# Hybrid attention and expert layers: the scores of two heads take turns on the two row halves of TensorE

## The chip, the cores and the metric

One core of a Trainium2 chip runs the whole program. The metric is the device time of one execution in microseconds, the median of several runs. TensorE multiplies matrices, VectorE (DVE), ScalarE (ACT) and GpSimd (POOL) work elementwise, and SyncE (SP) issues most transfers.

## The reference

Two layers run on 512 tokens of width 1024 (a grid of 8 rows by 64 columns). A layer projects the normalised input, runs three groups of heads (A: neighbourhood attention, 6 heads of 64; B: latent attention, 6 heads; C: a gated short convolution), projects their normalised outputs back onto `x`, and then runs a router with 16 experts. The change is in group A:

```python
def one_row(args):
    r, q_row = args
    r0 = jnp.clip(r - wh // 2, 0, rows - wh)
    k_win = lax.dynamic_slice_in_dim(kg, r0, wh, axis=1)[:, :, col_idx]
    v_win = lax.dynamic_slice_in_dim(vg, r0, wh, axis=1)[:, :, col_idx]
    ...
    sc = jnp.einsum('bqhd,biqjhd->bhqij', q_row, k_win).astype(jnp.float32) * scale
    sc = sc + bias.astype(jnp.float32)[None]
    p = jax.nn.softmax(sc.reshape(b, h, GRID_W, wh * ww), axis=-1).reshape(sc.shape).astype(v.dtype)
    return jnp.einsum('bhqij,biqjhd->bqhd', p, v_win)
```

## The kernel before

A layer is a mixer (the three groups of heads and the projections, `mixer`) and then the experts (`moe`). The tokens are in 4 blocks of 128, each block a stripe of 16 grid columns, so that a block's neighbourhood keys lie in 2 or 3 blocks (`KEYS_OF`): 256 or 384 score columns with a mask (`MASK_AT`).

To keep precision, matrices of the mixer are split into a high and a low part, and a product is three matmuls into one PSUM tile (`mm3`, L151 to L154): high x high (L152), low x high (L153), high x low (L154). The names of these three lines therefore appear for projections and for scores alike.

`a_attn` (L626 to L677) is neighbourhood attention. It goes over 3 pairs of heads (`hp`), 4 blocks of queries (`j`) and the 2 heads of a pair (`hh`). The queries and keys of the two heads of a pair lie in one tile, the first head in partitions 0 to 63, the second in 64 to 127; a score matmul therefore contracts over 64 rows and uses one row half of the array. For each head: GpSimd makes the masked bias (L642, once for each mask), three score matmuls go into an `sc` bank, VectorE adds the bias and takes the minimum (L655), ScalarE takes the exponential (L657), VectorE normalises (L659, L660), TensorE transposes in 2 or 3 pieces (L663, into the one `pt` bank) and VectorE or ScalarE copies them out (L665). When both heads are done, the `po` matmuls (L671) multiply with the values; they use half of the columns. There are two `sc` banks, one `pt`, one `po` and four `prj` banks.

What else stands in the same stretch: the last projections of `a_prep` (`prj<-wring,hn`, 384 columns), the output projection in three parts (`out_part`, L703: `prj<-...`, 512 columns, added to `x` in L712), the loads of its weights (`wo_loads`, L685: transfers L691 into `fraw`, ScalarE's cast L698, GpSimd's remainder L699), and the normalisations of the groups (`group_norm`, L363: one matmul with ones in L367, then L369 to L375). `weave` (L171) mixes these as fills between the steps of `a_attn`, at each `yield`. The first part of the output projection needs the convolution, the second group B, the third group A, so its last part waits for the normalisation at the end of `a_attn`.

The order in which an engine executes is not that of the source: a scheduler sets it when the program is built, from the order of the source, from priorities (`first` raises the steps of the woven main generator by 60) and from its own estimate of when operands and banks are ready. Each engine then executes its list in order and waits where an operand is late.

Of the kernel before, what the change touches and what calls it, by code (L numbers as in the profile page):

```python
# [93 lines left out]
def build(tc, x_in, pp_in, con_in, gm_in, rpb_in, w_in, w_uq, w_ukv, w_out, w_gate, w_up, w_down, out,  # L94
# [3 lines left out]
    PE, ACT, DVE, POOL, SP = nc.tensor, nc.scalar, nc.vector, nc.gpsimd, nc.sync  # L98
# [6 lines left out]
    def tmp():  # L105
        return w2.tile([128, 512], F32, name="tmp", tag="tmp")

    def stat(n, tag="stat"):
        return st.tile([128, n], F32, name=f"{tag}{n}", tag=f"{tag}{n}")
# [41 lines left out]
    def mm3(ps, ah, al, bh, bl, first, last):  # L151
        PE.matmul(ps, ah, bh, start=first, stop=False)  # L152
        PE.matmul(ps, al, bh, start=False, stop=False)  # L153
        PE.matmul(ps, ah, bl, start=False, stop=last)  # L154
# [41 lines left out]
    def psum(pool, tag, bufs):  # L196
        return lambda: pool.tile([128, 512], F32, name=tag, tag=tag, bufs=bufs)
# [17 lines left out]
    def mixer(l, M, W, PSUM):  # L215
        def ptile():
            return W.tile([128, 512], F32, name="P", tag="P", bufs=7)

        def ftile():
            return W.tile([128, 512], F32, name="tmf", tag="tmf", bufs=2)  # L220
# [28 lines left out]
        def qkA(which, part):  # L249

            return qk[which](part * 1536, 1536).rearrange("p (h t) -> p h t", h=3)
# [26 lines left out]
        prj, sc, ptb, pob = (psum(psm, n_, b_) for n_, b_ in zip(("prj", "sc", "pt", "po"), (4, 2, 1, 1)))  # L278
# [76 lines left out]
        def squares(o, tot):  # L355

            ACT.activation(tot, o[0], AF.Square)
            for i in range(1, len(o)):
                sq = tmp()
                ACT.activation(sq, o[i], AF.Square)  # L360
                DVE.tensor_tensor(tot, tot, sq, op=OP.add)

        def group_norm(bank, o, tot, k0, mix):  # L363

            n = len(o)
            pn = bank()
            PE.matmul(pn, ones, tot, start=True, stop=True)  # L367
            ln = tmp()
            ACT.activation(ln, pn, AF.Ln, scale=1.0 / (n * 128), bias=eps)  # L369
            ACT.activation(ln, ln, AF.Exp, scale=-0.5)  # L370
            for i in range(n):
                DVE.scalar_tensor_tensor(o[i], o[i], P("gout", k0 + i), ln, op0=OP.mult, op1=OP.mult)
                hi, lo = mix[i]
                ACT.copy(hi, o[i])
                DVE.tensor_tensor(lo, o[i], f(hi), op=OP.subtract)  # L375
# [250 lines left out]
        def a_attn():  # L626
            for hp in range(3):
                bms = [{}, {}]
                po = pob()
                for j in range(NJ):  # L630
                    k0, k1 = KEYS_OF[j]
                    n = (k1 - k0) * 128
                    pts = []
                    for hh in range(2):
                        h = 2 * hp + hh
                        rows = slice(hh * 64, hh * 64 + 64)
                        if MASK_AT[j] not in bms[hh]:

                            bm = ptile()
                            b0 = k0 - j + 1  # L640
                            m0 = _C["mask"][0] + MASK_AT[j]
                            POOL.tensor_tensor(  # L642
                                bm[:, 0:n].rearrange("p (b k w) -> p b k w", k=WH, w=CB),
                                bias[:, h].rearrange("p (k b w) -> p b k w", k=WH, b=3)[:, b0:b0 + k1 - k0],
                                con[:, m0:m0 + n // WH].rearrange("p (b k w) -> p b k w", k=1, w=CB)
                                .to_broadcast([128, k1 - k0, WH, CB]), op=OP.add)
                            bms[hh][MASK_AT[j]] = bm
                        bm = bms[hh][MASK_AT[j]]
                        ps = sc()
                        q = [qkA(0, p)[rows, hp, j * 128:(j + 1) * 128] for p in range(2)]  # L650
                        k = [qkA(1, p)[rows, hp, k0 * 128:k1 * 128] for p in range(2)]
                        mm3(ps[:, 0:n], q[0], q[1], k[0], k[1], True, True)
                        p = ftile()
                        nm = stat(1)
                        DVE.tensor_tensor_reduce(p[:, 0:n], ps[:, 0:n], bm[:, 0:n], -1.0, 3.0e38, OP.add, OP.min, nm)  # L655
                        s_ = stat(1)
                        ACT.activation(p[:, 0:n], p[:, 0:n], AF.Exp, bias=nm, scale=-1.0, accum_out=s_)  # L657
                        rl = stat(1)
                        DVE.reciprocal(rl, s_)  # L659
                        DVE.tensor_scalar(p[:, 0:n], p[:, 0:n], rl, None, op0=OP.mult)  # L660
                        pt = ptb()
                        for i in range(k1 - k0):
                            PE.transpose(pt[:, i * 128:(i + 1) * 128], p[:, i * 128:(i + 1) * 128], ident)  # L663
                        pT = tmp()
                        (ACT.copy if hh else DVE.tensor_copy)(pT[:, 0:n], pt[:, 0:n])  # L665
                        pts.append(pT)
                        yield
                    for i in range(k1 - k0):
                        for hh in range(2):
                            h = 2 * hp + hh  # L670
                            PE.matmul(po[hh * 64:hh * 64 + 64, j * 128:(j + 1) * 128],  # L671
                                      va[:, k0 + i, h * DH:(h + 1) * DH], pts[hh][:, i * 128:(i + 1) * 128],
                                      start=i == 0, stop=i == k1 - k0 - 1)
                ACT.copy(oA[hp], po)
            tot = tmp()
            squares(oA, tot)
            group_norm(sc, oA, tot, 0, mixA)  # L677
# [43 lines left out]
        for r in range(8):  # L721
            ACT.dma_start(bias[r * CB:(r + 1) * CB], rpb_in[l, :, :, (7 - r) * 48:(15 - r) * 48])
        weave(a_attn(), 40, (wl, 3, 0), (o1, 3, 4),
              (norm_later(sc, oB, F(0, 512), 3, mixB), 1, 0), (wl, 1, 0), (o1, 5 - 3, 4), (wl, 1, 0), (o1, 4, 4),
              (wl, 1, 0), (o2, 3, 3), (wl, 1, 0), (o2, 3, 3), (wl, 1, 0), (o2, 3, 3), (wl, 1, 0))
# [48 lines left out]
        for i, _ in enumerate(o3):  # L774
            j = i // 2
# [250 lines left out]
```

## Time and profile before

| | us |
|---|---|
| median of 3 runs | 1595.0 |
| lowest and highest | 1593.73, 1596.5 |
| the profiled execution | 1593.64 |
| its span, first to last instruction | 1591.9 |
| TensorE busy in it | 1549.4 |

The profile is of one execution. Its views give for each engine the busy time, the instructions in order of time with their start and length, what ended an engine's idle time, and busy time by stretch. A matmul's length includes its way through the array, so consecutive matmuls overlap in the rows; how fast they follow each other is read from the distance of their starts. The mean granted clock of TensorE is 0.991 of full speed.

### The profile page before, as it was taken

The numbers are of one execution on the slowest core, as the hardware profiler recorded it, in microseconds if no ns is written. First come the engines' busy times: TensorE is split into PE (matmuls) and PEld (weight loads), VectorE is DVE, ScalarE is ACT, GpSimd is POOL, SyncE is SP. The second block draws the span as 40 slices with busy tenths as digits, with TensorE's granted clock in tenths as the row PEclk, the third lists the DMA queues.
The fourth block names the chain that finished last, engine by engine and source line by source line (L and its number), as shares of the span: only waits on it lengthen the run. The fifth ranks groups of instructions, "written<-read, shape, count | busy, mean of one in ns | idle before, by whom it ended". The sixth has DMA issues, their size and how long they took to land. (4 is left out here: it accounts for less than half of the span.)

```text
span 1591.9 us, 19849 instructions
## 1 busy us (share of the span) xinstructions
PE 1549.4 (97%) x7820; PEld 845.5 (53%) x7822; DVE 512.6 (32%) x1142; ACT 382.1 (24%) x937; POOL 232.8 (15%) x336
## 2 busy tenths in 40 slices
PE   7999999899999999999999999999999999999997
PEld 6877766544444444344388776674344344344342
DVE  5475466511201201211164744664012022022021
ACT  6465553210000000000165655431100000000000
POOL 4541450200000000000055325320000000000000
PEclk8999999999999999999999999999999999999999
DMA  4312125799999999999622221187999999999966
GB/s 164 85 48 63 56 71 202 290 375 389 410 409 409 408 409 409 409 409 382 212 69 71 64 57 67 41 316 273 392 389 409 409 409 409 409 409 409 409 269 211
DMA packets 138461, 441.74 MB, mean 277 GB/s; under 512 B 8832, under 2 KB 31360, under 8 KB 138368
## 3 DMA queue, kind: packets, MB, share of 16 engines
q1 hardware_dynamic: 136576, 438.11, 71.6%
q10 hardware_dynamic: 1792, 2.36, 0.5%
q8 instruction: 62, 1.02, 0.3%
q14 instruction: 31, 0.25, 0.1%
HBM read 438.33 MB, written 2.10 MB: 277 GB/s over the span
## 5 line engine op out<-in xcount | busy, mean ns | idle before, releaser
L898 PE MATMUL acc<-w,fmix 128*64 128x512 f32 x2944 | 651.1, 595 | 0.0
L898 PEld LDWEIGHTS acc<-w,fmix 128*64 128x64 f32 x2944 | 203.5, 137 | 391.8 <-issue 368.8
L947 DVE TENSOR_TENSOR x<-wk,x 128x512 f32<-128x512 f32 x128 | 87.1, 689 | 273.9 <-PE wk L946 272.7
L888 PEld LDWEIGHTS wk<-tmp,fmix 128*128 128x128 f32 x1024 | 119.8, 192 | 42.4 <-issue 42.4
L932 ACT ACTIVATE tmp<-acc 128x512 f32<-128x512 f32 x32 | 19.1, 597 | 464.8 <-PE acc L898 382.2
L888 PE MATMUL wk<-tmp,fmix 128*128 128x128 f32 x1024 | 128.2, 279 | 0.7 <-DVE tmp L880 0.7
L926 POOL COPY sel<-con 16x128 f32<-16x128 f32 x16 | 5.0, 318 | 806.4 <-PE wk L927 800.0
L946 PE MATMUL wk<-tmp 128*128 128x512 f32 x256 | 114.7, 599 | 1.6 <-ACT tmp L942 1.6
L317 POOL TENSOR_TENSOR wring<-fraw,wring 128x384 fp32r<-128x384 f32 (+1 forms) x88 | 91.4, 1047 | 139.7 <-ACT wring L316 134.4
L890 DVE TENSOR_TENSOR fmix<-wk,pp 128x256 f32<-128x256 f32 (+1 forms) x72 | 28.4, 395 | 218.2 <-PE wk L888 218.2
L946 PEld LDWEIGHTS wk<-tmp 128*128 128x128 f32 x256 | 47.1, 190 | 68.9 <-issue 41.6
L153 PE MATMUL prj<-wring,hn 128*128 128x384 f32 (+1 forms) x224 | 80.6, 360 | 0.8 <-DVE hn L296 0.8
L152 PE MATMUL prj<-wring,hn 128*128 128x384 f32 (+1 forms) x224 | 79.8, 358 | 0.3 <-ACT wring L316 0.3
L154 PE MATMUL prj<-wring,hn 128*128 128x384 f32 (+1 forms) x224 | 79.3, 354 | 0.1
L942 ACT ACTIVATE tmp<-acc,stat 128x512 f32<-128x512 f32 x32 | 22.0, 687 | 214.5 <-PE acc L898 176.7
L933 DVE TENSOR_TENSOR tmp<-acc,tmp 128x512 f32<-128x512 f32 x32 | 22.1, 691 | 135.1 <-PE acc L898 135.1
L922 DVE COPY stat<-wk 64x1 f32<-64x1 f32 x32 | 5.0, 156 | 177.7 <-PE wk L919 177.5
L937 ACT COPY fmix<-wk 128x512 f32<-128x512 f32 x32 | 18.8, 587 | 179.1 <-PE wk L936 179.1
L316 ACT CAST wring<-fraw 128x384 fp32r<-128x384 f32 (+1 forms) x88 | 44.4, 513 | 39.8 <-PE prj L153 15.7
L153 PEld LDWEIGHTS prj<-wring,hn 128*128 128x128 f32 x224 | 43.0, 192 | 6.0 <-issue 3.9
L154 PEld LDWEIGHTS prj<-wring,hn 128*128 128x128 f32 x224 | 42.9, 192 | 5.2 <-issue 3.5
L152 PEld LDWEIGHTS prj<-wring,hn 128*128 128x128 f32 x224 | 42.9, 192 | 4.8 <-issue 3.0
(266 smaller groups left out, 2011.9 us busy)
## 6 DMA issues: line engine op xcount, KB each, us to landing
w<-in_w_gate_dram SPq DMA_DIRECT2D x128, 1024.0 KB, 14.4
w<-in_w_up_dram SPq DMA_DIRECT2D x128, 1024.0 KB, 18.2
w<-in_w_down_dram SPq DMA_DIRECT2D x112, 1024.0 KB, 13.5
w<-in_w_down_dram SPq DMA_DIRECT2D x32, 512.0 KB, 7.8
fraw<-in_w_in_dram SPq DMA_DIRECT2D x24, 384.0 KB, 3.2
fraw<-in_w_out_dram SPq DMA_DIRECT2D x16, 512.0 KB, 3.4
fraw<-in_w_in_dram SPq DMA_DIRECT2D x48, 128.0 KB, 2.4
fmix<-in_rpb_dram ACTq DMA_DIRECT2D x16, 144.0 KB, 3.4
```

The source lines that it names most:

```text
L152: PE.matmul(ps, ah, bh, start=first, stop=False)
L153: PE.matmul(ps, al, bh, start=False, stop=False)
L154: PE.matmul(ps, ah, bl, start=False, stop=last)
L316: ACT.copy(hi, raw[:, kk, :])
L317: POOL.tensor_tensor(lo, raw[:, kk, :], f(hi), op=OP.subtract)
L888: PE.matmul(pg[:, k * 128:(k + 1) * 128], xr[:, j, (k0 + k) * 128:(k0 + k + 1) * 128], og2[:, j, :], start=j == 0, stop=j == NJ - 1)
L890: DVE.tensor_tensor(xsT[:, k0:k0 + nk, :], pg[:, 0:nk * 128].rearrange("p (k s) -> p k s", k=nk), P("gffn")[:, k0:k0 + nk, None].to_broadc ...
L898: PE.matmul(ps[n][e * 64:(e + 1) * 64, :], lhs(k, e), w[:, e, n * 512:(n + 1) * 512], start=k == 0, stop=k == KC - 1)
L933: DVE.tensor_tensor(hid, U[n], hid, op=OP.mult)
L942: ACT.activation(ys, Y[n], AF.Copy, scale=gate)
L946: PE.matmul(po, osc[:, j * 128:(j + 1) * 128], ys, start=True, stop=True)
L947: DVE.tensor_tensor(x[:, j, c_], po, x[:, j, c_], op=OP.add)
```

## The change

The two heads of a pair are taken together. First the masked biases of both are made, then both take an `sc` bank, and the six score matmuls are written in turns: high x high of the first and of the second head, low x high of both, high x low of both. The rest of each head follows as before, the first head's softmax and transposes, a `yield`, the second head's. The matmuls, their operands and their sum are the same.

```diff
-                        rows = slice(hh * 64, hh * 64 + 64)
                         if MASK_AT[j] not in bms[hh]:
...
                             bms[hh][MASK_AT[j]] = bm
+
+                    pss = [sc(), sc()]
+                    for a, b in ((0, 0), (1, 0), (0, 1)):
+                        for hh in range(2):
+                            rows = slice(hh * 64, hh * 64 + 64)
+                            PE.matmul(pss[hh][:, 0:n], qkA(0, a)[rows, hp, j * 128:(j + 1) * 128],
+                                      qkA(1, b)[rows, hp, k0 * 128:k1 * 128], start=a + b == 0, stop=b == 1)
+                    for hh in range(2):
                         bm = bms[hh][MASK_AT[j]]
-                        ps = sc()
-                        q = [qkA(0, p)[rows, hp, j * 128:(j + 1) * 128] for p in range(2)]
-                        k = [qkA(1, p)[rows, hp, k0 * 128:k1 * 128] for p in range(2)]
-                        mm3(ps[:, 0:n], q[0], q[1], k[0], k[1], True, True)
+                        ps = pss[hh]
```

The scheduler orders the new source anew. The first place is TensorE at the start of `a_attn` in the first layer. `sc_2082` is the bank of the first head before; `sc_2084` and `sc_2085` are those of the first and the second head after; `prj_...` are projections over all 128 rows. Before:

```order
L152 MATMUL prj_1805<-wring_97,hn1_99 128x384
L153 MATMUL prj_1805<-wring_97,hn3_101 128x384
L154 MATMUL prj_1805<-wring_97,hn1_99 128x384
L152 MATMUL sc_2082<-qk1_103,qk0_102 128x256
L152 MATMUL prj_1806<-wring_97,hn1_99 128x384
L153 MATMUL sc_2082<-qk1_103,qk0_102 128x256
L153 MATMUL prj_1806<-wring_97,hn3_101 128x384
L154 MATMUL sc_2082<-qk1_103,qk0_102 128x256
L154 MATMUL prj_1806<-wring_97,hn1_99 128x384
```

After:

```order
L652 MATMUL sc_2084<-qk1_103,qk0_102 128x256
L153 MATMUL prj_1806<-wring_97,hn3_101 128x384
L652 MATMUL sc_2085<-qk1_103,qk0_102 128x256
L154 MATMUL prj_1806<-wring_97,hn1_99 128x384
L152 MATMUL prj_1807<-wring_97,hn1_99 128x384
L652 MATMUL sc_2084<-qk1_103,qk0_102 128x256
L652 MATMUL sc_2085<-qk1_103,qk0_102 128x256
L153 MATMUL prj_1807<-wring_97,hn3_101 128x384
L652 MATMUL sc_2084<-qk1_103,qk0_102 128x256
L154 MATMUL prj_1807<-wring_97,hn1_99 128x384
L652 MATMUL sc_2085<-qk1_103,qk0_102 128x256
```

The second head's scores moved up beside the first head's, but projections stand between most of the six. The same place on ScalarE, where the exponentials of the first two heads stand among casts of the output weights (`qk2_105<-fraw_104`). Before:

```order
L316 CAST wring_97<-fraw_104 128x384
L698 CAST qk2_105<-fraw_104 128x512
L657 ACTIVATE tmf_2086,stat1_2089<-tmf_2086,stat1_2087 128x256
L698 CAST qk2_105<-fraw_104 128x512 x3
L657 ACTIVATE tmf_2124,stat1_2127<-tmf_2124,stat1_2125 128x256
```

After:

```order
L316 CAST wring_97<-fraw_104 128x384
L702 CAST qk2_105<-fraw_104 128x512 x2
L661 ACTIVATE tmf_2092,stat1_2095<-tmf_2092,stat1_2093 128x256
L702 CAST qk2_105<-fraw_104 128x512
L661 ACTIVATE tmf_2124,stat1_2127<-tmf_2124,stat1_2125 128x256
```

Two casts instead of one stand ahead of the first exponential, and one instead of three between the two exponentials.

The second place is TensorE at the second pair of heads, first two groups. Before, `sc_2318` and `sc_2337` are the two heads of the first group and `sc_2360` is the first head of the second; after, the same are `sc_2320`, `sc_2321` and `sc_2362`. Before:

```order
L152 MATMUL sc_2318<-qk1_103,qk0_102 128x256
L153 MATMUL sc_2318<-qk1_103,qk0_102 128x256
L154 MATMUL sc_2318<-qk1_103,qk0_102 128x256
L152 MATMUL prj_2302<-qk2_105,lat_96 128x512
L153 MATMUL prj_2302<-qk2_105,lat_96 128x512
L154 MATMUL prj_2302<-qk2_105,lat_96 128x512
L152 MATMUL sc_2337<-qk1_103,qk0_102 128x256
L153 MATMUL sc_2337<-qk1_103,qk0_102 128x256
L154 MATMUL sc_2337<-qk1_103,qk0_102 128x256
L152 MATMUL sc_2360<-qk1_103,qk0_102 128x384
L153 MATMUL sc_2360<-qk1_103,qk0_102 128x384
L154 MATMUL sc_2360<-qk1_103,qk0_102 128x384
```

After:

```order
L652 MATMUL sc_2320<-qk1_103,qk0_102 128x256 x3
L152 MATMUL prj_2302<-qk2_105,lat_96 128x512
L153 MATMUL prj_2302<-qk2_105,lat_96 128x512
L154 MATMUL prj_2302<-qk2_105,lat_96 128x512
L652 MATMUL sc_2321<-qk1_103,qk0_102 128x256 x2
L652 MATMUL sc_2362<-qk1_103,qk0_102 128x384 x3
L652 MATMUL sc_2321<-qk1_103,qk0_102 128x256
```

The two heads of the group are not side by side here; the scheduler laid them apart nearly as before.

The third place is TensorE at the end of `a_attn`, where `sc_2724` is the matmul of the last normalisation (L367). Before:

```order
L154 MATMUL prj_2787<-hn1_99,lat_96 128x512
L152 MATMUL prj_2787<-wring_97,lat_96 128x512
L367 MATMUL sc_2724<-tmp_2716,ones_73 128x512
L153 MATMUL prj_2787<-wring_97,lat_96 128x512
L154 MATMUL prj_2787<-wring_97,lat_96 128x512
```

After:

```order
L154 MATMUL prj_2787<-hn0_98,lat_96 128x512
L367 MATMUL sc_2724<-tmp_2716,ones_73 128x512
L152 MATMUL prj_2787<-hn1_99,lat_96 128x512
L153 MATMUL prj_2787<-hn1_99,lat_96 128x512
L154 MATMUL prj_2787<-hn1_99,lat_96 128x512
L152 MATMUL prj_2787<-wring_97,lat_96 128x512
```

The normalisation moved up by four projections, which now stand behind it, ahead of the third part of the output projection.

## Rows read from the trace of the kernel before

**Rows 1.** The page, its first line of busy time, share and instructions by engine.

```profile
PE 1549.4 (97%) x7820; PEld 845.5 (53%) x7822; DVE 512.6 (32%) x1142; ACT 382.1 (24%) x937; POOL 232.8 (15%) x336
```

**Rows 2.** Busy time by stretch, columns in the first line: attention stage, expert stage.

```profile
core 0: us, PE busy (x) PEld busy (x) DVE busy (x) ACT busy (x) POOL busy (x), PEclk, DMA share, GB/s
190.00:270.00 80.00, 78.74 (x414) 51.67 (x413) 46.90 (x135) 37.12 (x91) 27.15 (x27) 1.00 0.31 112
...
440.00:500.00 60.00, 59.79 (x292) 25.85 (x290) 10.10 (x18) 3.74 (x6) 0.29 (x1) 1.00 1.03 409
```

**Rows 3.** Waits of SyncE's queue, 320 to 780 us: us in total, times, longest.

```profile
SPq L874 <- PE acc L898: 261.8, 132, 11.6
```

**Rows 4.** TensorE in order of time (start us, us, instruction): scores between projections.

```profile
190.29 0.33 PE L153 MATMUL prj<-wring,hn 128*128 128x384 f32 x1
190.46 0.34 PE L154 MATMUL prj<-wring,hn 128*128 128x384 f32 x1
...
191.04 0.44 PE L152 MATMUL prj<-wring,hn 128*128 128x384 f32 x1
...
191.72 0.44 PE L153 MATMUL prj<-wring,hn 128*128 128x384 f32 x1
192.09 0.38 PE L154 MATMUL sc<-qk,qk 64*128 64x256 f32 x1
```

**Rows 5.** TensorE in order of time: scores of both halves side by side.

```profile
198.65 0.44 PE L154 MATMUL sc<-qk,qk 64*128 64x384 f32 x1
198.65 0.43 PE L152 MATMUL sc<-qk,qk 64*128 64x384 f32 x1
199.01 0.45 PE L154 MATMUL prj<-wring,hn 128*128 128x384 f32 x1
...
199.76 0.45 PE L152 MATMUL prj<-wring,hn 128*128 128x384 f32 x1
```

**Rows 6.** TensorE in order of time: longer runs of scores.

```profile
219.82 0.38 PE L152 MATMUL sc<-qk,qk 64*128 64x256 f32 x1
220.04 0.28 PE L153 MATMUL sc<-qk,qk 64*128 64x256 f32 x1
220.16 0.27 PE L154 MATMUL sc<-qk,qk 64*128 64x256 f32 x1
...
221.26 0.45 PE L152 MATMUL sc<-qk,qk 64*128 64x256 f32 x2
...
221.98 0.50 PE L152 MATMUL prj<-qk,lat 128*128 128x512 f32 x1
...
222.92 0.33 PE L153 MATMUL sc<-qk,qk 64*128 64x384 f32 x1
223.10 0.33 PE L154 MATMUL sc<-qk,qk 64*128 64x384 f32 x1
223.36 0.44 PE L663 MATMUL pt<-con,tmf 128*128 128x128 f32 x2
```

**Rows 7.** TensorE in order of time: waits of the stage (idle and releaser in brackets).

```profile
194.25 0.34 PE L152 MATMUL prj<-wring,hn 128*128 128x384 f32 x1
195.76 0.41 PE L663 MATMUL pt<-con,tmf 128*128 128x128 f32 x2 [1.17 <-DVE tmf L660]
...
271.95 0.39 PE L154 MATMUL prj<-wring,lat 128*128 128x512 f32 x1
272.18 0.39 PE L152 MATMUL prj<-hn,qk 128*128 128x512 f32 x1
272.99 0.50 PE L153 MATMUL prj<-hn,qk 128*128 128x512 f32 x1 [0.43 <-DVE qk L375]
```

**Rows 8.** ScalarE and VectorE in order of time, ahead of the first transposes.

```profile
193.50 0.62 ACT L698 CAST qk<-fraw 128x512 fp32r<-128x512 f32 x1 [3.31 <-DMA fraw<-in_w_out_dram]
194.02 0.50 ACT L657 ACTIVATE tmf<-tmf,stat 128x256 f32<-128x256 f32 x1
...
194.85 0.76 DVE L660 TENSOR_SCALAR tmf<-tmf,stat 128x256 f32<-128x256 f32 x1
```

## Prediction

> **What bounds the kernel now.** I read the page first, then the windows, the queue of transfers, and last the order of time inside the attention stage. TensorE is busy for 97% of the span [rows 1], but such a number can hide pipelining, so the windows matter more: in the expert stage TensorE is busy 59.79 of 60 us, in the attention stage 78.74 of 80 us, while VectorE and ScalarE are there at 46.90 and 37.12 us [rows 2]. In the expert stage the queue that loads weights waits for TensorE to give buffers back (261.8 us in 132 waits [rows 3]), so what the attention stage loses or gains is handed on: the experts start later and nothing behind them has slack to take it up. TensorE executes its list in order, so time is made of two things: how long the list takes when nothing is missing, and the few places where an operand is late.
>
> The stage in question is `a_attn`, once per layer, in the first within the window of 190 to 270 us. Its 72 score matmuls (12 groups of two heads, three matmuls a head) contract over 64 rows and use half the array; their neighbours in the list, projections (`prj`) and transposes (`pt`), use all 128 rows.
>
> **The change, part by part.** Nothing is added to any engine: the same 72 matmuls a layer with the same shapes, the same weight loads, masks, softmax steps and transfers. What changes is the order, and it is not the one in the source: between the source and TensorE stands a scheduler, and the places in the section on the change show what it made of it.
>
> *Price of a run.* I call a run a row of score matmuls with no 128-row matmul between them. Two projections of 384 columns start 0.17 us apart (190.29, 190.46). With one score matmul of 256 columns between each two they start 0.68 us apart (191.04, 191.72) [rows 4]. One more score of 256 columns inside a run takes 0.12 us (220.04, 220.16) [rows 6]. So 0.68 - 0.17 - 0.12 = 0.39 us is paid for going into the half-array form and coming back, whatever is computed there. With 384 columns the same sum is 0.75 (199.01 to 199.76 [rows 5]) - 0.17 - 0.18 (222.92, 223.10 [rows 6]) = 0.40 us. The Trainium skill has the reason (TensorEngine Tiling (Array Packing), Key Properties): changing the tiling mode, though not changing the tile inside a mode, drains the engine. By that rule this change pays only if it makes fewer runs; the trace agrees, with 0.39 us for each, a price that the page doesn't give.
>
> *Number of runs.* Counted through the whole order of a layer, the scores stand in 31 runs before and in 38 after; single matmuls alone between full-height neighbours go from 11 to 19, whole heads of three from 13 to 11. The runs of `po` matmuls (half the columns) stay at 22. So 7 x 0.39 = +2.7 us a layer.
>
> *Pairs that overlap.* Where scores of both halves stand next to each other they do overlap: at 198.65 two start in the same 10 ns and the next projection starts 0.36 us later [rows 5], where two of one half would take about 0.18 + 0.36; that is 0.18 us saved. The block of six at 221.26 takes 0.72 us [rows 6] where one after the other would be 0.22 for the first (219.82, 220.04), 2 x 0.12, 2 x 0.18 and 0.26 for the way out (223.10, 223.36), 1.08 in all [rows 6]: 0.36 saved. Before, 4 runs a layer hold both halves (two like the first, two of the longer kind, near 1.0 us saved in all). After, 2 do: one pair of 256 columns (about 0.1) and one block of six (0.36). The change thus loses about +0.5 us of overlap a layer. The reason shows in the second place of the order: both heads take a score bank at once, there are two banks, and the second head's matmuls cannot stand before the previous group's second bank is read, so from the third group on the scheduler lays the heads apart again.
>
> *Waits.* Two waits of TensorE a layer can shrink, since the list is now longer. First, the transposes of the first head: they start 1.51 us after a projection that takes 0.18 (194.25, 195.76), so 1.33 us late [rows 7]. What they wait for starts with a transfer: ScalarE's cast waits for it until 193.50, the exponential follows at 194.02, VectorE's scaling at 194.85 [rows 8]. After, ScalarE has two casts ahead of that exponential instead of one (0.52 us, the distance of 193.50 and 194.02), and VectorE the reduction of the second head ahead of the scaling (most of which fits beside the exponential; I take 0.1). The transposes then can start at about 196.4. By the prices above the longer list reaches them at about 195.98 (third score of the first head at 193.14, then 2.84 us of list). About 0.45 to 0.6 us remain of the wait: -0.8 us. Second, the wait for the last group's normalised output (272.18 to 272.99 where projections of 512 columns are 0.23 apart, so 0.58 us [rows 7]): behind the normalising matmul L367 now stand 24 projections instead of 20, 4 x 0.23 = 0.9 us more cover, and as many as before (12) stand ahead of it behind the last `po`. That wait should go: -0.58 us. Elsewhere, by the same prices, more than 3.8 us of the new list lie between a head's last score and its transposes, more than the 3.67 us that the first head needs now (192.09 to 195.76). The one exception is the first head of the second pair: 3.2 us of list now (220.16 to 223.36 [rows 6]), about 2.4 after; there VectorE in the new order scales ahead of the other head's reduction, so I count nothing.
>
> *Sum.* A layer: +2.7 + 0.5 - 0.8 - 0.6 = +1.8 us; both layers have the same order, so +3.6 us. The profiled execution took 1593.64 us (1591.9 span and 1.7 around it), so it would be 1597.2; the median of the runs is 1595.0, 1.4 above it, and I put the forecast there: 1598.6 us, +0.23%.
>
> **Rivals.** *Not slower: the waits swallow the detours.* The place is the first transposes and the end of the stage. If the chain behind the first transfer isn't lengthened (the second cast and the other head's reduction fit beside it), all 1.33 + 0.58 = 1.91 us are absorbed: 2.7 + 0.5 - 1.9 = +1.3 us a layer, 1596.2 for the profiled execution and 1597.6 on the median, no change that can be told. It decides at 195.98 us: if the transposes' operand is there by then, this rival holds. For it: the detours lie ahead of the waits. Against it: ScalarE's cast of 0.52 us stands straight on that chain.
>
> *Slower: the waits move along.* The first head's third score comes 1 us later than before (193.14 for 192.09), so if its softmax is as slow as now from there, 3.67 us, the wait stays near 0.8 to 1.3, and if ScalarE or VectorE reach the last group's output later by what the list grew, so does the last one. Then +3.2 us a layer is left whole: 1600.0, on the median 1601.4.
>
> *The change does what it says.* If all 36 pairs of a layer stood side by side in 12 runs, 19 runs would fall away (7.4 us) and each pair would save about 0.1 to 0.18 (some 4 us): -11 us a layer, 1572. For its condition speaks the Trainium skill (TensorE: Matmul & The Clock Gate, Part 3): matmuls on different row groups run side by side, the next weights loading meanwhile; the rows at 198.65 bear that out [rows 5]. But the order holds 2 such runs a layer. A gain of over 0.2% would need overlap across a full-height matmul, and the spacing of 0.68 us in [rows 4] shows none.
>
> **How the numbers follow.** 0.2%, 3.2 us, is about what a measurement of this kernel can tell from no change. Forecast 0.47, of which 0.05 would come out under 3.2 us; waits swallow it 0.33; waits move along 0.13; real pairing 0.04; something else that ends near zero 0.03. So faster 0.04, same 0.41, slower 0.55. The range runs from 1594.9 (all waits absorbed and part of a run's price hidden, near no change) to 1602.6 (nothing absorbed and a new wait of 0.6 us in each layer: 2 x 3.8). I don't widen it to the pairing rival.
>
> **What would show it.** Right: the alternating stretch at 191 to 194 us with projections 0.68 us apart round single scores; more runs at the same price; first transposes near 196.4; no wait before the second matmul of the third output part near 273; each attention stage 1.5 to 2 us longer and the expert stages as long as before. Wrong: heads that overlap although a projection stands between them, a run that costs much less than 0.39 us, or an expert stage that takes the delay back because its weights had been late.

## The result and the profile after

The changed kernel took 1609.3 us in the median of 20 runs (1597.2 to 1620.7), against 1595.1 us for the kernel before in 20 runs beside it (1593.5 to 1599.6): a ratio of 1.0092, 95% interval 1.0076 to 1.0107. It is slower, by 14 us where 3.6 were forecast, outside the range. Its runs also spread over 23 us, those of before over 6. The profiled execution took 1616.5 us; its span of 1614.7 us is 22.8 us above that of before.

The page of after, busy time by engine (answers to [rows 1]), and the granted clock in 40 slices of the span:

```profile
PE 1574.1 (97%) x7822; PEld 858.6 (53%) x7822; DVE 508.7 (32%) x1142; ACT 381.8 (24%) x937; POOL 236.3 (15%) x336
...
PEclk8999979999999999999999998899999999999999
```

TensorE has 25 us more of busy time for the same matmuls (7822 records, 7820 before), and the clock row shows where: three slices below 9 inside the run, one in the first layer, two in the second. Busy time by stretch of after (columns in the first line, PEclk is the granted clock as a share of full speed; [rows 2] before):

```profile
core 0: us, PE busy (x) PEld busy (x) DVE busy (x) ACT busy (x) POOL busy (x), PEclk, DMA share, GB/s
190.00:200.50 10.50, 9.58 (x37) 5.88 (x37) 3.04 (x10) 3.91 (x10) 6.85 (x7) 1.00 0.47 152
200.50:221.00 20.50, 20.50 (x65) 13.41 (x65) 6.60 (x20) 6.92 (x17) 9.35 (x8) 0.50 0.23 78
221.00:270.00 49.00, 49.00 (x262) 30.51 (x261) 31.22 (x98) 21.42 (x56) 10.97 (x11) 1.00 0.12 41
440.00:500.00 60.00, 59.78 (x291) 25.76 (x290) 9.97 (x19) 3.74 (x6) 0.28 (x1) 1.00 1.03 409
965.10:968.50 3.40, 3.40 (x15) 2.11 (x14) 2.34 (x7) 1.66 (x5) 0.00 (x0) 0.50 0.02 5
995.80:1019.70 23.90, 23.90 (x71) 15.12 (x72) 5.97 (x20) 7.54 (x18) 10.77 (x10) 0.50 0.20 67
```

From 200.5 to 221.0 us TensorE is granted 1.2 GHz instead of 2.4, and from 995.8 to 1019.7 us in the second layer again, both times in `a_attn`; a short stretch at 965 us lies ahead of it, in code that the change doesn't touch. In [rows 2] the clock is 1.00 in both stretches. The expert stage is as before: 291 matmuls in 60 us.

TensorE of after in order of time, around the fall (start us, us, instruction; idle and releaser in brackets):

```profile
190.24 0.44 PE L153 MATMUL prj<-wring,hn 128*128 128x384 f32 x1
190.61 0.38 PE L652 MATMUL sc<-qk,qk 64*128 64x256 f32 x1
190.92 0.45 PE L154 MATMUL prj<-wring,hn 128*128 128x384 f32 x1
...
194.82 0.34 PE L152 MATMUL prj<-wring,hn 128*128 128x384 f32 x1
196.08 0.41 PE L667 MATMUL pt<-con,tmf 128*128 128x128 f32 x2 [0.92 <-DVE tmf L664]
...
199.52 0.45 PE L152 MATMUL prj<-wring,hn 128*128 128x384 f32 x1
199.90 0.44 PE L652 MATMUL sc<-qk,qk 64*128 64x384 f32 x1
200.26 0.50 PE L153 MATMUL prj<-wring,hn 128*128 128x384 f32 x1
200.69 0.69 PE L652 MATMUL sc<-qk,qk 64*128 64x384 f32 x1
...
201.80 0.52 PE L152 MATMUL prj<-wring,hn 128*128 128x384 f32 x1
202.12 0.52 PE L153 MATMUL prj<-wring,hn 128*128 128x384 f32 x1
...
203.18 0.69 PE L154 MATMUL prj<-wring,hn 128*128 128x384 f32 x1
...
204.42 0.69 PE L152 MATMUL prj<-wring,hn 128*128 128x384 f32 x1
```

I call a score matmul alone between projections a single, and the way from the projection ahead of it to the one behind it a detour. At full clock projections round a single of 256 columns stand 0.68 us apart (190.24, 190.92), as in [rows 4]; round one of 384 columns 0.74 (199.52, 200.26), as in [rows 5]. Behind 200.5 us the same detour takes 1.24 (203.18, 204.42), and two projections in a row are 0.32 apart (201.80, 202.12) where [rows 4] have 0.17. So ahead of the fall TensorE did four things: four singles and a pair between projections, ten projections in a row (the last at 194.82), an idle 0.92 us, and singles again.

**Where the 22.8 us are.** From the first matmul of group B's scores to the first expert matmul (L888 before, L892 after) of the first layer it is 213.9 us before (97.78 to 311.69) and 224.3 after (96.83 to 321.14); from the last of these expert matmuls in the first layer to the first in the second it is 347.1 (749.36 to 1096.49) and 361.2 (758.83 to 1119.99). That is +10.4 and +14.0 us; the rest of the program is 1.6 us shorter, mostly at its start. At half clock stand 20.5 + 23.9 + 3.4 = 47.8 us that before doesn't have in these stretches. How much of them is lost is read where the same list runs at full clock (the sixth experiment): 109 matmuls in the same stretch instead of 65, so work goes at 65/109 = 0.60 of its speed and about 0.40 x 47.8 = 19 us are lost. Some 24.4 - 19 = 5 us are then left for the longer list, 2.6 us a layer.

The profiled execution is 7 us slower than the median, so the split of the 14 us is another. The mean granted clock is known of each, and time goes with it: over the 20 executions of after, from 0.991 at 1597.2 us to 0.975 at 1620.7, one us more at half clock goes with about 0.36 us more of time (correlation 0.90). In the median after has 0.983; before has 0.989 to 0.991 in the medians of its executions beside the experiments. That is some 0.007 x 2 x 1609 = 23 us more at half clock and, at 0.40, about 9 of the 14 us, an estimate; the other 5 are again the list.

### The profile page after: what moved, and what is told of

The parts are those of the page before. It is cut to its first block, busy times and chain, and to the rows that moved or that the text cites. A ratio compares the mean times of both kernels' runs of the same rounds, so it can differ in the third digit from the quotient of the medians.

```text
span 1614.7 us, 19849 instructions
## 1 busy us (share of the span) xinstructions
PE 1574.1 (97%) x7822; PEld 858.6 (53%) x7822; DVE 508.7 (32%) x1142; ACT 381.8 (24%) x937; POOL 236.3 (15%) x336
## 5 line engine op out<-in xcount | busy, mean ns | idle before, releaser
L892 PEld LDWEIGHTS wk<-tmp,fmix 128*128 128x128 f32 x1024 | 119.8, 192 | 42.4 <-issue 42.4
L892 PE MATMUL wk<-tmp,fmix 128*128 128x128 f32 x1024 | 128.2, 279 | 0.7 <-DVE tmp L884 0.7
L153 PE MATMUL prj<-wring,hn 128*128 128x384 f32 (+1 forms) x224 | 83.6, 373 | 0.8 <-DVE hn L296 0.8
L154 PE MATMUL prj<-wring,hn 128*128 128x384 f32 (+1 forms) x224 | 83.2, 371 | 0.2 <-POOL wring L317 0.2
L152 PE MATMUL prj<-wring,hn 128*128 128x384 f32 (+1 forms) x224 | 82.5, 370 | 0.4 <-ACT wring L316 0.4
L154 PEld LDWEIGHTS prj<-wring,hn 128*128 128x128 f32 x224 | 45.0, 201 | 6.4 <-issue 4.8
L153 PEld LDWEIGHTS prj<-wring,hn 128*128 128x128 f32 x224 | 44.8, 200 | 6.8 <-issue 4.3
L152 PEld LDWEIGHTS prj<-wring,hn 128*128 128x128 f32 x224 | 44.6, 199 | 5.8 <-issue 4.3
```

The costliest lines, as they stand in the source:

```text
L892: PE.matmul(pg[:, k * 128:(k + 1) * 128], xr[:, j, (k0 + k) * 128:(k0 + k + 1) * 128], og2[:, j, :], start=j == 0, stop=j == NJ - 1)
```

## The experiments

**Without the half-array form.** First after, then before, with all scores over 128 rows:

```diff
-                            rows = slice(hh * 64, hh * 64 + 64)
+                            rows = slice(0, 128)
```

> The kernel after, with every score contracted over 128 rows instead of 64, so that both heads of a pair give the same mixture; that changes what is computed. 72 score matmuls a layer in the same places by the source, none in the half-array form. Theory 1 (the many changes of the array's form among the projections make the loss: directly through 0.39 us for each run, and through the granted clock that falls to half in the attention stage after them): no fall of the clock in either attention stage, TensorE's spacing round a single score 0.29 us instead of 0.68, and 31 x 0.39 = 12 us a layer less than before, less about 1 us of overlap and up to 2 us of waits that come back: 1573 to 1580 us. Rival (the clock falls because scores stand ahead of and between the projections, whatever their form, or because of the wait for the first transposes): the clock falls again near 200 us, and the time is about 12 us above that, 1585 to 1592.

Measured: 1585.0 us, ratio 0.9936 (0.9925 to 0.9948).

> The kernel before, with every score contracted over 128 rows instead of 64 (both heads of a pair then give the same mixture; that changes what is computed). It is to the kernel before what the first experiment is to the kernel after. Theory 1 (what the alternation costs is the form changes and what they do to the clock): with no half-array form the two sources give the same time, within 0.2% of the 1585.0 us of that run, 1582 to 1588, with at most short falls of the clock in the attention stages. Rival (the alternating order itself costs, by the banks that it holds and the waits that follow): this one is faster than 1585 by a good part of the 14 us that lie between before and after, 1571 to 1579.

Measured: 1584.4 us, 0.9928 (0.9915 to 0.9942). Without the half-array form both orders take the same time (0.6 us apart): the alternation costs nothing without the form. The gain of the first run is smaller than the 15 to 22 us expected, at the edge of its rival's range, and its trace shows why. TensorE of it in order of time, then by stretch (columns as above):

```profile
190.46 0.28 PE L652 MATMUL sc<-qk,qk 128*128 128x256 f32 x1
190.57 0.34 PE L153 MATMUL prj<-wring,hn 128*128 128x384 f32 x1
...
193.62 0.34 PE L152 MATMUL prj<-wring,hn 128*128 128x384 f32 x1
196.56 0.41 PE L667 MATMUL pt<-con,tmf 128*128 128x128 f32 x2 [2.61 <-DVE tmf L664]
```

```profile
197.80:201.30 3.50, 3.50 (x14) 3.33 (x13) 0.71 (x3) 0.65 (x2) 2.51 (x2) 0.51 0.34 130
```

A score costs its 0.11 us and nothing for the form (190.46, 190.57). But TensorE now reaches the first transposes earlier and waits 2.61 us there, and behind that wait the clock falls too, as the rival had it, though for 3.4 us only. No detours stand behind it; that they are what holds the clock down in after is how I read it. From 150 us to the first expert matmul TensorE is idle for 9.0 us instead of 6.7, and the clock (10.2 us at half instead of 3.4) takes about 3 us more than before; with the 4.8 us that the layer is shorter, the list has shrunk by some 10 us for 31 runs, and with the 1.0 us of overlap lost that is 0.35 us a run, near the 0.39 of the prediction.

**The same half for both heads.**

```diff
-                            rows = slice(hh * 64, hh * 64 + 64)
+                            rows = slice(0, 64)
```

> The kernel after, with the scores of both heads taken from row half 0; that changes what is computed (the second head repeats the first). Same 38 runs a layer, same order, but no score lies on the other half. Theory 1 (runs of the half-array form bring the clock down, on which half they lie doesn't matter): the clock falls to half near 200 us and again in the second layer's attention stage, about 20 us each, time near that of after, 1604 to 1615 (overlap of about 0.5 us a layer lost as well). Rival (what costs is going from one row half to the other): the clock holds, projections round a single score stand closer than 0.68 us, time 1592 to 1598.

Measured: 1609.9 us (1597.4 to 1621.8), 1.0069 (1.0043 to 1.0095), the clock at 0.50 from 200.7 and from 999.4 us for 23.8 us each. On which half the scores lie plays no part that can be told; the detours are between half-height and full height.

**Scores kept together.** Six, then three matmuls of a run as one piece:

```diff
+                    with tc.tile_critical():
                         (the six matmuls of a pair; in the other kernel mm3 of each head)
```

> The kernel after, with the six score matmuls of a pair kept together on TensorE: 12 runs a layer, all of six, alternating between the halves, instead of 38. Same half-height matmuls in number and shape. Theory 1 (runs are what costs, and their crowding is what takes the clock): the clock holds in both attention stages; 19 runs fewer than before x 0.39 = 7.4 us a layer less, and 11 more blocks of six that save 0.36 us of overlap each, 4 less the 1.0 of before, so 3 us: -10 us a layer, if no new wait comes; each block needs both score banks free, which can cost up to 0.5 us a block, so 1575 to 1587. Rival (half-height matmuls, or scores moved up, bring the clock down themselves): the clock falls to half near 200 us or near the blocks, 1587 to 1600.

Measured: 1643.4 us, 1.0302 (1.0283 to 1.0320).

> The kernel before, with the three score matmuls of each head kept together: 24 runs a layer of three, no run with both halves. Theory 1, by its price: 7 runs fewer x 0.39 = -2.7 us a layer, +1.0 us of overlap lost, so -1.7 us a layer: 1591 to 1593 us, the clock as in before. Rival (a run's price is hidden in waits or differs with its neighbours, so the count of runs doesn't set the time): 1595 or above.

Measured: 1698.8 us, 1.0652 (1.0638 to 1.0665). Both expectations failed, and not in a way that tells the theories apart. TensorE of the first of them in order of time:

```profile
191.74 0.34 PE L153 MATMUL prj<-wring,hn 128*128 128x384 f32 x1
197.21 1.01 PE L653 MATMUL sc<-qk,qk 64*128 64x256 f32 x6 [5.14 <-DMA fraw<-in_w_out_dram]
198.15 0.69 PE L154 MATMUL prj<-wring,hn 128*128 128x384 f32 x1
```

The runs are as few as meant (six scores in one row), but a piece kept together this way starts late: 5.14 us of idle time ahead of this one, 28.6 us from 150 us to the experts, where before has 6.7, and 32.0 us with three at a time. The clock falls after these waits several times. Fewer runs are worth nothing if they are bought with waits; whether they pay without them was not shown this way.

**Without the wait** (the sixth experiment). ScalarE's first casts of the output weights are queued behind the first head's exponential; the names are those of the code, and the lines that keep the first exponential in `first_exp` are left out:

```diff
...
-                        ACT.copy(hi[:, c_], raws[i - 1][:, c_])
+                        with tc.issue_after(first_exp[0]):
+                            ACT.copy(hi[:, c_], raws[i - 1][:, c_])
```

> The kernel after, with ScalarE's casts of the output projection's weights put behind the first head's exponential, so that the first transposes (idle 0.92 us at 196.08 us in after) have their operand before TensorE reaches them. TensorE's order in 190 to 200 us stays as it is but for the transposes of the second head, which come one score earlier. Theory 1a (the wait tips the clock, the crowd of short single scores only keeps it low): no fall of the clock in the first layer's attention stage, 1595 to 1599 us. Theory 1b (the crowd of single scores between projections is enough): the clock falls to half near 200 us all the same for about 20 us, 1604 to 1612.

Measured: 1599.75 us in 11 runs (1598.2 to 1604.9), 1.0030 (1.0020 to 1.0039). By stretch (columns as above), then TensorE of the second layer in order of time:

```profile
189.00:200.50 11.50, 11.50 (x51) 8.04 (x49) 3.30 (x10) 4.06 (x10) 7.88 (x8) 1.00 0.31 96
200.50:221.00 20.50, 20.32 (x109) 13.10 (x110) 10.78 (x31) 11.37 (x27) 16.07 (x16) 1.00 0.41 136
```

```profile
984.82 0.34 PE L152 MATMUL prj<-wring,hn 128*128 128x384 f32 x1
984.99 0.38 PE L671 MATMUL pt<-con,tmf 128*128 128x128 f32 x2
...
985.66 0.43 PE L654 MATMUL sc<-qk,qk 64*128 64x384 f32 x1
986.02 0.44 PE L152 MATMUL prj<-wring,hn 128*128 128x384 f32 x1
...
986.76 0.44 PE L153 MATMUL prj<-wring,hn 128*128 128x384 f32 x1
```

The transposes follow the projection without idle time, the projections round the singles behind them stand 0.74 apart as in after (986.02, 986.76), there are 40 runs a layer instead of 38, and the clock stays at 1.00 in `a_attn` of both layers. Some 10 of the 14 us are gone, and not in one execution alone: 1 of 11 took over 1602 us here, 18 of 20 in after. With nearly the same crowd of singles, taking the wait of about 1 us away takes the long fall away, nearly every time; the kernel with the same half for both heads and that of the next experiment, whose profiles have the long fall too, wait there as well (0.80 and 0.97 us). The edit also adds two runs and moves the second head's transposes up by one score, so the wait is not its only difference. The run also gives the price of the list by itself: its two stretches, measured as above, are 3.2 and 4.3 us longer than before, each with a 3.4 us fall ahead of `a_attn` that takes about 1.4, so 1.8 and 2.9 us a layer.

**The first pair of heads alone.**

```diff
+ALT = (0,)
...
-                    pss = [sc(), sc()]
+                    pss = [sc(), sc()] if hp in ALT else []
... (the other two pairs with mm3, head after head, as before)
```

> Alternating scores for the first pair of heads alone, the other two pairs head after head as before: 37 runs a layer, TensorE's order as in after up to about 221 us and close to that of before behind it. Theory 1 (the loss is the clock that falls in the first pair's stretch, where single scores stand between projections): as slow as after, 1604 to 1612, the clock at half from about 200 us. Rival (the loss comes with alternation wherever it stands, by runs and waits): about a third of the 14 us, 1598 to 1601, no fall of the clock.

Measured: 1609.2 us (1601.0 to 1621.1), 1.0085 (1.0054 to 1.0117); the clock is at 0.50 from 201.2 and from 999.9 us for 23.9 us each. Its profile is of its slowest execution. The whole loss is there with a third of the alternation: it lies in the stretch where the first pair's scores stand between projections.

**A longer wait in before.**

```diff
                     SP.dma_start(raws[i], w_out[l, ks[i] * 128:(ks[i] + 1) * 128, :])
+                    if i == 0:
+                        SP.dma_start(raws[i][:, 0:128], w_out[l, ks[i] * 128:(ks[i] + 1) * 128, 0:128])
```

> The kernel before, with a second, small transfer into the buffer of the first output weights (the first 128 columns once more), so that ScalarE's cast and the first head's exponential behind it come later. TensorE's order is that of before up to the scores behind the first transposes; from there five more scores of the first pair stand alone between projections (34 runs instead of 31). The scores of the two heads do not alternate. Theory 1a (a wait ahead of a crowd of single scores brings the clock down, and the crowd keeps it there; alternation matters only as it makes the crowd): the wait at the first transposes grows from 1.17 to 2 to 3.5 us, the clock falls to half at about 198 to 201 us for 10 us or more in both layers, 1603 to 1618 us. Rival (alternating halves is needed for the long fall): the wait costs itself, 1 to 2.5 us a layer, and at most a short fall of 3.4 us (1.7 us lost), 1597 to 1602.

Measured: 1602.3 us (1599.1 to 1610.4), 1.0040 (1.0023 to 1.0057), between the two ranges. The wait didn't grow; TensorE in order of time:

```profile
196.65 0.41 PE L663 MATMUL pt<-con,tmf 128*128 128x128 f32 x2 [1.19 <-DVE tmf L660]
```

So it tells nothing of a longer wait. What it had was three runs more a layer; in the profiled execution, its fastest at 1599.1 us, the clock holds in `a_attn` in spite of the wait of 1.19 us, and each stretch is about 3 us longer than before, of which a 3.4 us fall ahead of `a_attn` takes some 1.4 and the runs 1.2. In other executions the mean clock is down to 0.982 and the time up to 1610; no profile shows where.

**Before without its wait.** The same edit as above on the kernel before:

> The kernel before, with ScalarE's casts of the first output weights put behind the first head's exponential, as in the sixth experiment for after. By the rows of before the wait at the first transposes (1.17 us) goes: -1.1 us a layer, one run more (32): +0.4, two more runs of output matmuls; so 1593 to 1595 us, and the clock holds in the attention stages. Rival (the wait only moves to the next group, or the changed order makes a new one): 1596 or above.

Measured: 1596.7 us in 12 runs (1592.9 to 1607.6), 1.0007 (0.9988 to 1.0026): above the 1593 to 1595 expected, and no change that can be told. Six runs lie at 1592.9 to 1594.6, but two at 1605.6 and 1607.6 with a mean clock of 0.98. The wait is worth its 1 us a layer at best, and taking it away doesn't make the clock safe in every run.

**Both banks early, but head after head.** The two loops of the scores exchanged:

```diff
-                    for a, b in ((0, 0), (1, 0), (0, 1)):
-                        for hh in range(2):
+                    for hh in range(2):
+                        for a, b in ((0, 0), (1, 0), (0, 1)):
```

> Both score banks taken and both heads' scores issued ahead of both softmaxes, as in after, but head after head: three matmuls of the first head, then three of the second, no alternation by the source. TensorE's order as scheduled has 40 runs a layer (22 single scores), the first pair's stretch as crowded as in after. Theory 1 (the crowd of single scores behind the wait takes the clock, and it comes from holding both banks early, not from alternating): as slow as after, 1604 to 1613, with falls of the clock in the attention stages. Rival (alternation itself is what costs): 1595 to 1600.

Measured: 1603.3 us (1598.4 to 1610.4), 1.0049 (1.0032 to 1.0066): just below the 1604 to 1613 of the theory and above the 1595 to 1600 of the rival. TensorE in order of time:

```profile
193.75 0.38 PE L652 MATMUL sc<-qk,qk 64*128 64x256 f32 x1
194.06 0.44 PE L152 MATMUL prj<-wring,hn 128*128 128x384 f32 x1
194.43 0.38 PE L652 MATMUL sc<-qk,qk 64*128 64x256 f32 x1
194.74 0.57 PE L153 MATMUL prj<-wring,hn 128*128 128x384 f32 x1
195.10 0.53 PE L154 MATMUL prj<-wring,hn 128*128 128x384 f32 x1
...
198.38 0.33 PE L154 MATMUL prj<-wring,hn 128*128 128x384 f32 x1
```

By stretch (columns as above):

```profile
190.00:194.90 4.90, 4.90 (x19) 2.90 (x18) 0.43 (x2) 1.41 (x4) 1.58 (x2) 1.00 0.69 212
194.90:198.30 3.40, 3.40 (x12) 3.31 (x13) 1.52 (x6) 2.00 (x6) 3.40 (x4) 0.50 0.01 5
```

This corrects the theory. The clock falls at 194.9 us, behind six singles, with no wait ahead of it and no idle time in the rows: the crowd alone can do it. It comes back at 198.3, after a row of projections; it falls again among the next singles at 205.1, and in the second layer from 993.6 to 1014.1. A wait isn't needed, then, but neither does the same crowd bring a fall each time: in the second layer of this very execution the same six singles stand between 981.99 and 985.88 us, and the clock holds until 993.6. That in after the crowd and the wait add up is how I read the three kernels together; no run varies the wait alone. The profile here is of the slowest execution of seven.

**Full height without leaving anything out.** The keys of each head are kept in 128 rows, the other head's 64 rows zero; the second copy goes into parts of `qk0`, `qk1` and `lat` that are free by then (helper `kz`). The first version (a later expectation calls it the eighth experiment):

```diff
...
-                        q = [qkA(0, p)[rows, hp, j * 128:(j + 1) * 128] for p in range(2)]
-                        k = [qkA(1, p)[rows, hp, k0 * 128:k1 * 128] for p in range(2)]
+                        q = [qkA(0, p)[:, hp, j * 128:(j + 1) * 128] for p in range(2)]
+                        k = [kz_all(hh, p, hp)[:, k0 * 128:k1 * 128] for p in range(2)]
```

> A version for use: the kernel before, with each head's keys held in 128 rows of which the other head's 64 are zero, so that every score matmul has 128 rows and nothing is left out. It costs 16 more small copies a layer in the preparation of the keys and four fills with zeros on GpSimd. Theory 1: the time of the 128-row version of before (1582 to 1588) plus little, 1582 to 1590, faster than both kernels. Rival (the new copies delay the attention stage, or the clock falls as the waits grow): 1592 or above.

Measured: 1592.9 us, 0.9983 (0.9974 to 0.9991), above the expected 1582 to 1590, where the rival had put it. TensorE in order of time:

```profile
168.25 0.50 PE L152 MATMUL sc<-qk 96*128 96x512 f32 x1 [0.87 <-ACT P L577]
...
170.99 0.79 PE L152 MATMUL sc<-qk 96*128 96x512 f32 x1 [1.77 <-ACT P L577]
```

The added copies delay ScalarE in group B's attention, TensorE waits for its exponential (L577), and the clock falls behind that (the matmul at 170.99 takes 0.79 us, the one at 168.25 0.50). The last version moves the copies to GpSimd and takes the cast out of the way:

```diff
+                    split_out(pv, qkA(1, 0)[:, :, t], qkA(1, 1)[:, :, t], g=gab[:, 0:1])
...
+                    for p in range(2):
+                        k_ = f(qkA(1, p)[LOW, :, t])
+                        for a, b in ((0, 2), (2, 3)):
+                            POOL.tensor_copy(kz(LOW, p, a, b)[:, :, t], k_[:, a:b])
+                        POOL.memset(k_, 0.0)
...
```

> The zero-padded keys again (every score matmul over 128 rows, nothing left out), with two changes: the halves of the second head are copied and zeroed by GpSimd behind the old two copies, so that the score bank of the preparation comes free as early as in before, and the casts of the first output weights stand behind the first head's exponential. The version of the eighth experiment lost 0.87 and 1.77 us in waits of TensorE near 168 and 171 us, a clock fall of 3.41 us there (1.7 us lost), and 2.29 us at the first transposes. If these go, 1592.9 - 2 x (2 + 1.7 + 1.3) = 1583, 1580 to 1588, about the time of the 128-row version that leaves the padding out (1584.4). Rival (GpSimd's copies delay its share of the weights and TensorE waits for that): 1590 or above.

Measured: 1585.3 us (1583.9 to 1589.3), 0.9932 (0.9916 to 0.9948): 10 us faster than before and 24 faster than after, the fastest of the kernels that leave nothing out. TensorE in order of time:

```profile
195.44 0.34 PE L154 MATMUL prj<-wring,hn 128*128 128x384 f32 x1
195.99 0.41 PE L700 MATMUL pt<-con,tmf 128*128 128x128 f32 x2 [0.21 <-DVE tmf L697]
...
197.66 0.34 PE L152 MATMUL sc<-qk,qk 128*128 128x384 f32 x1
197.83 0.33 PE L152 MATMUL prj<-wring,hn 128*128 128x384 f32 x1
```

The score takes 0.17 us and leaves no gap, and of the 2.29 us of wait 0.21 is left. The waits near 169 us did not all go: 0.87 us is left at 167.51 and 0.46 us at 168.93, and in the first layer the clock is at half behind them from 169.2 to 176.1 us, longer than the 3.41 us that the expectation counted away; in the second layer there is no such fall. So the time came as expected with one of its three terms failing in one layer.

## Why the prediction failed, point by point

- *Price of a run, 0.39 us.* Right: 0.68 and 0.74 round a single [rows 4, 5], and 0.35 worked out from the first kernel without the form.
- *31 to 38 runs, +2.7 us, and the lost overlap, +0.5 us.* The count is that of the order. For the sixth experiment the same sum gives 9 runs x 0.39 + 0.5 - 1.33 - 0.58 = 2.1 us a layer, and 1.8 and 2.9 were measured. The term for the overlap alone can't be told: with no pair on two halves the time was the same (1609.9 for 1609.3).
- *Wait at the first transposes, 1.33 to about 0.5 us.* Too hopeful: 0.92 us idle at 196.08, which is 196.08 - 194.82 - 0.18 = 1.08 us by the prediction's own measure. The list reached them when it should have (the layer runs 0.95 us ahead of that of before, 96.83 for 97.78, so the 195.0 us here stand for 195.95, and 195.98 was forecast); their operand came 0.6 us late. The chain of [rows 8] in after:

```profile
192.57 1.14 ACT L702 CAST qk<-fraw 128x512 fp32r<-128x512 f32 x2 [3.35 <-DMA fraw<-in_w_out_dram]
193.61 0.50 ACT L661 ACTIVATE tmf<-tmf,stat 128x256 f32<-128x256 f32 x1
```

```profile
194.36 0.43 DVE L659 CUSTOM_DVE_ANT_0 tmf<-sc,P 128x256 f32<-128x256 f32 x1
194.71 1.22 DVE L664 TENSOR_SCALAR tmf<-tmf,stat 128x256 f32<-128x256 f32 x1
```

  The two casts and the second head's reduction stand where they were put; the reduction puts the scaling off by 0.27 us (it starts 0.47 us behind the reciprocal ahead of it, before 0.20) where 0.1 was taken, and the scaling took 1.22 us; in [rows 8] it took 0.76, in the sixth experiment 0.35. In the two slow cases GpSimd makes the weights' remainder beside all of it (L703, from 193.26 to 195.78 us in after), in the fast one only from 195.90 on, when the scaling has begun (195.81). That this is the cause was not tested.
- *Wait at the end of the stage, 0.58 us, gone.* Right, the two matmuls that stood 0.81 us apart in [rows 7] stand 0.23 apart:

```profile
282.38 0.39 PE L152 MATMUL prj<-hn,qk 128*128 128x512 f32 x1
282.61 0.39 PE L153 MATMUL prj<-hn,qk 128*128 128x512 f32 x1
```

- *The sum.* Here is the step that failed: it was made at full clock from end to end. [Rows 2] show 1.00 for the stage before, and the prediction kept that for the new list without asking whether it holds there. There was no term for the clock and no rival with it. The runs showed 20.5 and 23.9 us at half clock in the two attention stages of the profiled execution, which at 0.40 cost about 18 of its 22.8 us, and about 9 of the median's 14 us by the mean clocks. The rival in which the waits swallow the detours (1597.6) is refuted by the wait that stayed. The one in which the waits move along (1601.4) had the first wait right, 0.8 to 1.3 us, and the last one wrong; neither has the fall. What is left without it, near 1600 us (1599.75 in the sixth experiment), lies inside the range.
- *What would show it.* The spacing of 0.68 us, the 38 runs, the end of the stage without a wait and the expert stages as long as before came as forecast. The transposes at 196.08 look like the forecast 196.4, but that is luck: on the time of before it is 197.03. The stages grew by 10 and 14 us instead of 1.5 to 2. None of the three signs of being wrong came, and none of them looked at the clock.

What stays open: why the clock falls in some executions of a kernel and not in others (after from 1597.2 to 1620.7 us, before without its wait from 1592.9 to 1607.6), why the same six singles bring it down in one layer of an execution and not in the other, and why several profiles have a short fall ahead of `a_attn` in code that those kernels leave as it was. Only one execution of each kernel has a profile, and those of after, of the same half, of the first pair alone and of head after head are slower than their medians.

## What to carry to other kernels

Where a sum over a TensorE stage is made, the granted clock of that stage belongs into it as a term of its own: ask whether the change thins out what the array does, by waits or by detours, and price the stage at half clock as a rival. Work on half of the array costs two changes of form each time it is put between full-height matmuls; padding the operand with zeros to full height can be cheaper than the half array (1585.3 us here, against 1595.8 before beside it). And before the source's order is taken for the engine's, the scheduled order has to be looked at.

## What the runs showed of the hardware

- A TensorE that is never idle in the rows can lose half its clock: at 194.9 us in the kernel with head after head, behind six singles that alternate with projections, each pair 0.68 us long for some 0.29 us of columns (0.17 + 0.12). The Trainium skill (TensorE: Matmul & The Clock Gate, A second HAM failure mode: psum-queue depth-cycling) describes a kernel whose many short idle times between groups of matmuls make the clock go back and forth. The clock goes back and forth here too (down at 194.9, up at 198.3, down at 205.1 us), but behind detours and without idle time ahead of the first fall; whether it is the same cause no run here shows.
- Half clock doesn't double everything: projections in a row went from 0.17 to 0.32 us, the detour round a single from 0.74 to 1.24 us, the stretch as a whole to 0.60 of its speed. The same page (Terms) takes half of the time spent at half clock as the loss, 23.9 us for the 47.8 us here as an estimate. The rows give about 19, and the 20 executions 0.36 us for each us at half clock.
- Without the half-array form 256 score columns between projections take 0.11 us (190.46 to 190.57), against 0.51 us with it (0.68 - 0.17).
